# The last recurrent head of a hybrid decoder layer: from seven block sizes one at a time to two block sizes per step

## The chip, the core and the metric

The kernel runs on one core of a Trainium2 chip. The core has five engines that each take their instructions strictly in the order in which the program lists them: TensorE (PE, with its weight loads shown apart as PEld), VectorE (DVE), ScalarE (ACT), GpSimd (POOL) and SyncE (SP, which here issues the DMAs). They meet only through semaphores: an instruction that needs another engine's result waits at the head of its own queue, and everything behind it waits too. The metric is the device time of one execution in microseconds (us), here the median of three runs.

## The reference

One layer of batch 1, 1024 positions, width 1024, all in float32: a norm, one projection `h @ w_in` into attention (8 heads of 64) and a recurrence (4 heads of 128), an output projection, a norm and residual, and a feed-forward block of 4096. The part that matters here is the recurrence of one head:

```python
def step(state, xs):
    qc, kc, vc, gc = xs
    b = jnp.cumsum(gc, axis=2)
    o_inter = jnp.einsum('bhtk,bhkv->bhtv', qc * jnp.exp(b), state)
    diff = b[:, :, :, None, :] - b[:, :, None, :, :]
    decay = jnp.exp(jnp.where(causal, diff, -jnp.inf))
    a = jnp.einsum('bhtk,bhsk,bhtsk->bhts', qc, kc, decay)
    o = o_inter + jnp.einsum('bhts,bhsv->bhtv', a, vc)
```

The decay between two positions depends on the channel, so `a` is no plain matrix product. A kernel can still make it from products if it joins neighbouring blocks: for blocks of c positions, the queries of the upper block carry the decay from the block's start, the keys of the lower block the decay to the block's end, and one product gives all pairs between the two. Doubling c from 1 to 64 gives every pair inside 128 positions.

## The kernel before

All large products use float32r operands in a high and a low part, three matmuls for one (lines 90 to 92). The kernel has three stages: the input projections with the four recurrent heads among them, the attention with the output projection, and the feed-forward block.

The order of the work is written out by hand. `hgrn_core(h)` (line 501) emits the recurrence of head h, and at chosen places calls `fill(ns)` (line 195), which takes that much work, by fixed prices, from a queue of generators. For heads 0 to 2 the queue holds the projections of the next recurrent head (`hgrn_ig`, `hgrn_qf`); for the last head, h = 3, it holds the projections of attention pairs 0 and 1 (`attn_proj`, line 785). One item of those is three matmuls of 128x512, priced at 650; eight items make one half (512 positions) of a projection, in a PSUM bank of the tag "mm", of which there are two. `attn_proj(0)` yields the queries (tile `pm_aq`, two halves), the first half of the values (`pm_av`), the keys (`pm_ak`, two halves) and the second half of the values.

What an item leaves to the other engines matters below. A finished half is read out of PSUM by DVE (`qf` at line 806, `vf` at line 823, `kf` at line 740), and ACT and POOL split it into a high and a low part (lines 733 and 734), which SP sends on by DMA (lines 750, 811 and 812). The weights of the next projection are split by ACT (`wh`, line 86) and DVE (`wl`, line 87). The values are turned by four PE transposes (`pvt`, line 773), which need `vf`; ACT and DVE read the result (lines 776 and 777).

Inside `hgrn_core`, `qt` and `kt` are the queries and keys of the head (channels x positions), `tot` the decays of the blocks, `at` the matrix `a` of each 128 positions, and `pd` two ones-products for its diagonal (line 510). There are two ways to climb the block sizes:

- Heads 0 to 2 take three steps with c = 1, 4 and 16 (lines 520 to 571), each doing the sizes c and 2c. `quarter_sets` (line 472) prepares for each half of the positions a tile `qs` of 192 columns per 128 positions, by two ACT copies (lines 483 and 487) and two DVE products (lines 488 and 490). Eight matmuls of 128x192 (`pl`, line 529) go to four PSUM banks, DVE scales `qt` and `kt` and multiplies the decays (lines 542 to 556), prepares the next sets, and then writes `at` by twelve predicated copies (line 561). After each step come two fills of 3500. Size 64 follows as eight matmuls of 64x64 (line 572) and two DVE products.
- The last head takes the seven sizes of `LEVELS` one at a time (lines 585 to 613): eight matmuls of 128x64 (line 593), one DVE product each for `kt` (line 597) and `qt` (line 599), the decays (line 603), one predicated copy for all of `at` (line 604), and a fill of 3700, 2900 or 2200.

All fills of the last head are multiplied by the `scale` of 1.15 that is handed to it. After the sizes the keys are transposed (`pk`, line 615), the state is carried (`pu`, `st`) and the output formed (`po`).

A float32 product counts as two PE instructions, so eight of them are 16 in the trace.

Of the kernel before, what the change touches and what calls it, by code (L numbers as in the profile page):

```python
# [37 lines left out]
def hymba_layer(ctx, tc, x, w_in, w_out, w_ff1, w_ff2, g_pre, lb_logits, g_mix, g_post,  # L38
# [156 lines left out]
    def fill(ns, least=False):  # L195
        debt[0] += ns
        if least:
            debt[0] = max(debt[0], 1.0)
        while debt[0] > 0 and queue:
            try:  # L200
                cost = next(queue[0])
            except StopIteration:
                queue.pop(0)
                continue
            if cost is None:
                break
            debt[0] -= cost
        debt[0] = min(debt[0], 0.0)
# [292 lines left out]
    def hgrn_core(h, scale, after=None):  # L501
        hd = heads[h]
        inat, gate, prod, qt, kt, tot = (hd[n] for n in ("inat", "gate", "prod", "qt", "kt", "tot"))
        ready = quarter_sets(hd, h, 0, tot) if h < HH - 1 else None
        fill((5900 if 0 < h < HH - 1 else 5200) * scale)
        at = slab("S", f"at{h}", F32, (P, NT, P))
        for hf in range(2):
# [7 lines left out]
            nc.sync.dma_start(out=gcols, in_=g_mix.rearrange("(k p) -> p k", p=P))  # L515
        if h == HH - 1:
            load_bias(0)
        if h < HH - 1:
            fill(1200 * scale)
            totals = slab("P", f"tot{h}")  # L520
            for step in range(3):
                c = 4 ** step
                nb = 32 // c
                sets, cv = ready
                banks4 = []
                for u in range(4):
                    pl = bank(("s", "t", "pv")[(2 * step + u // 2) % 3], f"pl{h}_{step}{u}").rearrange("p (n q) -> p n q", n=2)
                    for n in range(2 * u, 2 * u + 2):
                        TE.matmul(pl[:, n % 2, :192], kt[:, n * P:(n + 1) * P], sets[u // 2][:, n % 4],  # L529
                                  start=True, stop=True)  # L530
                    banks4.append(pl)
                w = T // (4 * c)
                at_ = (0, 768, 960)[step]
                tots = totals[:, at_:at_ + 3 * w].rearrange("p (i w) -> p i w", i=3)
                u23, u123, nx = (tots[:, i] for i in range(3))
                cw = cv.rearrange("p n b f -> p (n b) f")
                q4 = qt.rearrange("p (m f c) -> p m f c", f=4, c=c)
                k4 = kt.rearrange("p (m f c) -> p m f c", f=4, c=c)

                def spread(ap, k=c):  # L540
                    return ap.unsqueeze(2).to_broadcast([P, w, k])
                V.tensor_tensor(out=q4[:, :, 1], in0=q4[:, :, 1], in1=spread(cw[:, :, 0]), op=ALU.mult)
                for hf in range(2):
                    n4 = slice(hf * 4, hf * 4 + 4)
                    V.tensor_tensor(out=qt[:, hf * 512:hf * 512 + 512].rearrange("p (n b f c) -> p n b (f c)", n=4, f=4, c=c)
                                    [:, :, :, 2 * c:],
                                    in0=sets[hf][:, :, 128:].rearrange("p n (b w) -> p n b w", b=nb),
                                    in1=cv[:, n4, :, 0:1].to_broadcast([P, 4, nb, 2 * c]), op=ALU.mult)
                V.tensor_tensor(out=u23, in0=cw[:, :, 2], in1=cw[:, :, 3], op=ALU.mult)
                V.tensor_tensor(out=u123, in0=cw[:, :, 1], in1=u23, op=ALU.mult)  # L550
                V.tensor_tensor(out=nx, in0=cw[:, :, 0], in1=u123, op=ALU.mult)
                if step < 2:
                    ready = quarter_sets(hd, h, step + 1, nx)
                V.tensor_tensor(out=k4[:, :, 2], in0=k4[:, :, 2], in1=spread(cw[:, :, 3]), op=ALU.mult)
                V.tensor_tensor(out=k4[:, :, 1], in0=k4[:, :, 1], in1=spread(u23), op=ALU.mult)
                V.tensor_tensor(out=k4[:, :, 0], in0=k4[:, :, 0], in1=spread(u123), op=ALU.mult)
                for u, pl in enumerate(banks4):
                    for part_, mask, c2 in ((0, masks[:, 2 * step], c), (2, masks[:, 2 * step + 1], 2 * c),
                                            (1, near[:, step], 2 * c)):
                        av = at[:, 2 * u:2 * u + 2].rearrange("p n (b two c) -> p n b two c", two=2, c=c2)  # L560
                        V.copy_predicated(
                            av[:, :, :, 1, :],
                            mask.rearrange("p (b c) -> p b c", c=c2).unsqueeze(1).to_broadcast([P, 2, 64 // c2, c2]),
                            pl[:, :, part_ * 64:part_ * 64 + 64].rearrange("p n (b c) -> p n b c", c=c2))
                cur = nx
                table_part()
                fill(3500 * scale)
                table_part()
                fill(3500 * scale)
            pl = bank("s", f"pl{h}_6")  # L570
            for n in range(NT):
                TE.matmul(pl[:64, n * 64:(n + 1) * 64], kt[:, n * P:n * P + 64], qt[:, n * P + 64:(n + 1) * P],
                          start=True, stop=True)
            S.activation(at[:64, :, 64:], pl[:64].rearrange("p (n c) -> p n c", n=NT), AF.Copy)
            kv, qv = (x.rearrange("p (n two c) -> p n two c", two=2, c=64) for x in (kt, qt))
            cv = cur.rearrange("p (n two) -> p n two", two=2)
            V.tensor_tensor(out=qv[:, :, 1], in0=qv[:, :, 1], in1=cv[:, :, 0:1].to_broadcast([P, NT, 64]), op=ALU.mult)
            V.tensor_tensor(out=kv[:, :, 0], in0=kv[:, :, 0], in1=cv[:, :, 1:2].to_broadcast([P, NT, 64]), op=ALU.mult)
            nx = tp.tile([P, NT], F32, tag="tot8", name=f"tot{h}_8", bufs=1)
            V.tensor_tensor(out=nx, in0=cv[:, :, 0], in1=cv[:, :, 1], op=ALU.mult)  # L580
            cur = nx
            fill(3400 * scale)
        else:
            cur = tot
            fill(1200 * scale)
            for li, c in enumerate(LEVELS):
                nb = 64 // c
                qv = qt.rearrange("p (b two c) -> p b two c", two=2, c=c)
                kv = kt.rearrange("p (b two c) -> p b two c", two=2, c=c)
                av = at.rearrange("p n (b two c) -> p n b two c", two=2, c=c)  # L590
                pl = bank("s", f"pl{h}_{li}")
                for n in range(NT):
                    TE.matmul(pl[:, n * 64:(n + 1) * 64], kt[:, n * P:(n + 1) * P],
                              qv[:, n * nb:(n + 1) * nb, 1, :], start=True, stop=True)
                w = T // (2 * c)
                cv = cur[:, :2 * w].rearrange("p (b two) -> p b two", two=2)
                V.tensor_tensor(out=kv[:, :, 0, :], in0=kv[:, :, 0, :],
                                in1=cv[:, :, 1:2].to_broadcast([P, w, c]), op=ALU.mult)
                V.tensor_tensor(out=qv[:, :, 1, :], in0=qv[:, :, 1, :],
                                in1=cv[:, :, 0:1].to_broadcast([P, w, c]), op=ALU.mult)  # L600
                nx = slab("P", f"tot{h}_{w}") if w > 32 else \
                    tp.tile([P, w], F32, tag=f"tot{w}", name=f"tot{h}_{w}", bufs=1)
                V.tensor_tensor(out=nx[:, :w], in0=cv[:, :, 0], in1=cv[:, :, 1], op=ALU.mult)
                V.copy_predicated(
                    av[:, :, :, 1, :],
                    masks[:, li].rearrange("p (b c) -> p b c", c=c).unsqueeze(1).to_broadcast([P, NT, nb, c]),
                    pl.rearrange("p (n b c) -> p n b c", n=NT, c=c))
                cur = nx
                fill((3700 if li == 0 else 2900 if li < 3 else 2200) * scale)
        ktr = slab("T", f"ktr{h}", F32, (P, NT, P))  # L610
        for hf in range(2):
            pt = bank("t", f"pk{h}_{hf}")
# [1699 lines left out]
```

## Time and profile before

| what | value |
|---|---|
| median of 3 runs | 1205.58 us (1205.57 to 1205.9) |
| the profiled execution, from outside | 1205.52 us |
| its span, first to last instruction | 1203.5 us |
| outside the span | 2.0 us |
| mean granted TensorE clock | 0.999 |
| the last head, from its `pd` to the end of its `pu` | 249.5 to 292.6 us |

Times inside the span count from its first instruction. A row of a timeline has the start, the length, the engine, the source line, the operation with the tile that it writes and the tiles that it reads, the shape and the count; an ending in brackets is the idle time before it and what ended that. Ends of matmuls are modelled and overlap the next one's start, so what a matmul costs is read from start to start.

### The profile page before, as it was taken

What the parts mean: (1) busy time and instruction counts of PE and PEld (TensorE: products, weight loads), DVE (VectorE), ACT (ScalarE), POOL (GpSimd) and SP (SyncE); (2) the same over time, 40 slices, a digit from 0 to 9 for tenths busy, and PEclk for the clock granted to TensorE, in tenths of its full rate; (3) what the DMA queues carried; (4) which work ended last, traced back from release to release, by engine and by line L of the source; (5) the groups of instructions that cost most, each with busy time, mean ns of one, the idle gap of its engine ahead of it and who ended that gap; (6) DMA issues with size and microseconds to landing.
All of it is one profiled execution on the core that took longest, in us unless ns stands there. A gap on an engine that the chain in (4) does not pass through costs nothing.

```text
span 1203.5 us, 17310 instructions
## 1 busy us (share of the span) xinstructions
PE 1195.3 (99%) x6342; PEld 1025.7 (85%) x6342; DVE 849.7 (71%) x1438; ACT 542.3 (45%) x1065; POOL 294.7 (24%) x280
## 2 busy tenths in 40 slices
PE   9999999999999999999999999999999999999997
PEld 9898989888888888888888888888888888888886
DVE  5696978775666767676599665766687553578796
ACT  7633333321565668855664222222234543434562
POOL 0121112010111110153421787575531000000022
PEclk9999999999999999999999999999999999999999
DMA  5222323135545556272524465553587534523337
GB/s 218 71 68 84 96 85 95 50 100 123 156 107 129 130 150 153 57 244 103 192 75 163 165 229 184 182 206 135 201 326 269 183 105 140 173 89 105 105 105 279
DMA packets 90547, 175.46 MB, mean 146 GB/s; under 512 B 14944, under 2 KB 42464, under 8 KB 90464
## 3 DMA queue, kind: packets, MB, share of 16 engines
q1 hardware_dynamic: 90320, 174.37, 45.6%
q8 instruction: 50, 0.82, 0.3%
q14 instruction: 33, 0.27, 0.1%
q10 hardware_dynamic: 144, 0.00, 0.0%
HBM read 116.91 MB, written 47.99 MB: 137 GB/s over the span
## 4 chain that ended last, share of the span: by engine, by line
PE 96%; ACT 2%; DVE 1%; issue 1%; DMA 0%; POOL 0%; DVEq 0%; POOLq 0%; ACTq 0%
PE f L2052 18%; PE f2s L2052 7%; PE pig L92 2%; PE pig L90 2%; PE pig L91 2%; PE pl L529 2%; PE pwo L90 2%; PE pwo L92 2%; PE pwo L91 2%; PE pm_ak L90 1%; PE pm_aq L90 1%; PE pm_f L90 1%; PE pm_aq L92 1%; PE pm_ak L92 1%; PE pm_ak L91 1%; PE pm_aq L91 1%
## 5 line engine op out<-in xcount | busy, mean ns | idle before, releaser
L87 DVE TENSOR_TENSOR al<-ar,ah 128x1024 fp32r<-128x1024 f32 x56 | 70.6, 1261 | 80.4 <-ACT ah L86 80.2
L2052 PE MATMUL f<-bh,ah 128*128 128x512 f32 x320 | 124.5, 389 | 0.0
L2052 PE MATMUL f<-bl,ah 128*128 128x512 f32 x320 | 124.5, 389 | 0.0
L2052 PE MATMUL f<-bh,al 128*128 128x512 f32 x320 | 124.5, 389 | 0.0
L86 ACT ACTIVATE ah<-ar 128x1024 fp32r<-128x1024 f32 x56 | 59.1, 1056 | 86.6 <-DMA ar<-actd 84.3
L2052 PEld LDWEIGHTS f<-bl,ah 128*128 128x128 f32 x320 | 60.1, 188 | 12.6
L2052 PEld LDWEIGHTS f<-bh,al 128*128 128x128 f32 x320 | 60.1, 188 | 12.5
L2052 PEld LDWEIGHTS f<-bh,ah 128*128 128x128 f32 x320 | 60.1, 188 | 12.3
L2126 POOL TENSOR_SCALAR lbl<-ssq 128x1 f32<-128x1 f32 x4 | 3.3, 820 | 245.7 <-ACT fd L2122 245.5
L1675 POOL TENSOR_TENSOR e<-x,e 128x512 f32<-128x512 f32 x14 | 21.6, 1541 | 131.0 <-DVE x L1626 123.8
L2052 PE MATMUL f2s<-bl,ah 128*128 128x512 f32 (+1 forms) x128 | 48.9, 382 | 0.0
L2052 PE MATMUL f2s<-bh,al 128*128 128x512 f32 (+1 forms) x128 | 48.9, 382 | 0.0
L2052 PE MATMUL f2s<-bh,ah 128*128 128x512 f32 (+1 forms) x128 | 48.9, 382 | 0.0
L718 POOL TENSOR_SCALAR tout<-traw 128x256 f32<-128x256 f32 x16 | 18.4, 1150 | 107.0 <-DMA traw<-in_bias_tab_dram 107.0
L87 DVE TENSOR_TENSOR bl<-br,bh 128x1024 fp32r<-128x1024 f32 x32 | 40.1, 1253 | 1.3 <-ACT bh L86 1.2
L2069 ACT ACTIVATE acc<-f 128x512 f32<-128x512 f32 x28 | 16.7, 598 | 49.5 <-PE f L2052 49.5
L86 ACT ACTIVATE bh<-br 128x1024 fp32r<-128x1024 f32 x32 | 33.6, 1050 | 4.3 <-PE f L2052 2.7
L87 DVE TENSOR_TENSOR wl<-raw,wh 128x1024 fp32r<-128x1024 f32 x21 | 25.9, 1233 | 10.2 <-ACT wh L86 10.2
L764 POOL TENSOR_TENSOR kl<-kf,kh 64x512 fp32r<-64x512 f32 x12 | 15.4, 1287 | 70.9 <-ACT kh L763 49.4
L90 PE MATMUL pwo<-woh,mt 128*128 128x512 f32 x80 | 32.2, 402 | 0.0
L92 PE MATMUL pwo<-woh,mt 128*128 128x512 f32 x80 | 31.3, 391 | 0.0
L91 PE MATMUL pwo<-wol,mt 128*128 128x512 f32 x80 | 31.2, 390 | 0.0
(1724 smaller groups left out, 3937.7 us busy)
## 6 DMA issues: line engine op xcount, KB each, us to landing
ar<-actd SPq DMA_DIRECT2D x56, 512.0 KB, 3.6
br<-in_w_ff_dram SPq DMA_DIRECT2D x16, 1024.0 KB, 5.8
raw<-in_w_in_dram SPq DMA_DIRECT2D x28, 512.0 KB, 4.1
w1r<-in_w_ff_dram SPq DMA_DIRECT2D x14, 1024.0 KB, 6.5
actd<-e SPq DMA_DIRECT2D x17, 768.0 KB, 4.3
actd<-e SPq DMA_DIRECT2D x11, 1024.0 KB, 4.1
xr<-in_x_dram SPq DMA_DIRECT2D x8, 512.0 KB, 8.0
raw<-in_w_out_dram SPq DMA_DIRECT2D x8, 512.0 KB, 3.7
```

The lines of the kernel that those rows point to most:

```text
L86: S.activation(hi, src, AF.Copy)
L87: eng.tensor_tensor(out=lo, in0=src, in1=f32(hi), op=ALU.subtract)
L90: TE.matmul(dst, lhs[0], rhs[0], start=start, stop=False)
L91: TE.matmul(dst, lhs[0], rhs[1], start=False, stop=False)
L92: TE.matmul(dst, lhs[1], rhs[0], start=False, stop=stop)
L529: TE.matmul(pl[:, n % 2, :192], kt[:, n * P:(n + 1) * P], sets[u // 2][:, n % 4], start=True, stop=True)
L718: G.tensor_scalar(by_class(dst[:, part_ * w:(part_ + 1) * w]), in_blocks(raw[:, FAR * DIL:]), 8.0, None, op0=ALU.mult)
L764: G.tensor_tensor(out=kl[a:b], in0=src, in1=f32(kh[a:b]), op=ALU.subtract)
L1675: eng[0].tensor_tensor(out=e1[:, 3], in0=a21, in1=e1[:, 2], op=ALU.add)
L2052: TE.matmul(pm, a[:, j, c], b[:, j, d], start=start and j == 0 and q == 0, stop=stop and j == 1 and q == 2, skip_group_check=True)
L2069: S.activation(acc_at(p, i), pm, AF.Copy)
L2126: G.tensor_scalar(base[:, t:t + 1], sums[j][:, t:t + 1], 1.0 / D, EPS, op0=ALU.mult, op1=ALU.add)
```

## The change

The branch of the last head is taken out, and all four heads take three steps of two sizes, then size 64. The last head's `scale` goes from 1.15 to 1.0, so that its fills sum to 39400 where they were 38295. Lines move up by one inside the function and by 28 behind it; the body of the three steps is the same, only its indentation changes.

```diff
-        ready = quarter_sets(hd, h, 0, tot) if h < HH - 1 else None
+        ready = quarter_sets(hd, h, 0, tot)
         fill((5900 if 0 < h < HH - 1 else 5200) * scale)
...
-        if h < HH - 1:
-            fill(1200 * scale)
-            totals = slab("P", f"tot{h}")
-            for step in range(3):
...
-        else:
-            cur = tot
-            fill(1200 * scale)
-            for li, c in enumerate(LEVELS):
...
-                pl = bank("s", f"pl{h}_{li}")
-                for n in range(NT):
-                    TE.matmul(pl[:, n * 64:(n + 1) * 64], kt[:, n * P:(n + 1) * P],
-                              qv[:, n * nb:(n + 1) * nb, 1, :], start=True, stop=True)
...
-                cur = nx
-                fill((3700 if li == 0 else 2900 if li < 3 else 2200) * scale)
+        fill(1200 * scale)
+        totals = slab("P", f"tot{h}")
+        for step in range(3):
...
+            table_part()
+            fill(3500 * scale)
+            table_part()
+            fill(3500 * scale)
+        pl = bank("s", f"pl{h}_6")
...
+        fill(3400 * scale)
...
-        last_gate = hgrn_core(h, 1.15 if last else 1.0, open_attention if last else None)
+        last_gate = hgrn_core(h, 1.0 if last else 1.0, open_attention if last else None)
```

`table_part` has done all its parts in heads 0 to 2 and returns at once in the last head.

Three places show what this does to the queues. The first is ACT at the start of the last head, before the change (`texp` only fetches the table of the exponential, `wh_2742` are the weights of the first values):

```order
L1312 ACT_TABLE_LOAD
L1312 ACTIVATE texp<-nhalf 128x1
L86 ACTIVATE wh_2742<-raw_2499 128x1024
L469 ACTIVATE rc_2751<-rrow 128x512
L470 ACTIVATE rrow<-rc_2751 128x512
```

The same place after the change:

```order
L1284 ACT_TABLE_LOAD
L1284 ACTIVATE texp<-nhalf 128x1
L483 ACTIVATE qs_00_2726<-qt_2501 128x4x64
L487 ACTIVATE qs_00_2726<-qt_2501 128x4x32
L483 ACTIVATE qs_01_2731<-qt_2501 128x4x64
L487 ACTIVATE qs_01_2731<-qt_2501 128x4x32
L86 ACTIVATE wh_2752<-raw_2499 128x1024
```

Four copies for the first sets stand behind the table load and ahead of the weights.

The second place is DVE between the weights of the keys (`wl_2862`) and the turned values (`v_2830`), before the change:

```order
L87 TENSOR_TENSOR wl_2862<-raw_2607,wh_2861 128x1024
L597 TENSOR_TENSOR kt_2588<-kt_2588,tot_256_2849 128x128x4
L599 TENSOR_TENSOR qt_2501<-qt_2501,tot_256_2849 128x128x4
L603 TENSOR_TENSOR tot_128_2884<-tot_256_2849 128x128
L604 COPY_PREDICATED at_2778<-masks,pl_2_2873 128x128x4
L823 TENSOR_TENSOR vf_2890<-pm_av_2831,rrow 128x512
L777 TENSOR_TENSOR v_2830<-pvt_2909,v_2830 128x8x64
```

The same stretch after the change begins with the twelve copies of step 0, of which the last is shown; `vf_2945` ends it:

```order
L560 COPY_PREDICATED at_2781<-near,pl_03_2809 128x64x2
L778 TENSOR_TENSOR qf_2861<-pm_aq_2792,rrow 128x512
L87 TENSOR_TENSOR wl_2888<-raw_2607,wh_2887 128x1024
L541 TENSOR_TENSOR qt_2501<-qt_2501,tot_2799 128x64x4
L544 TENSOR_TENSOR qt_2501<-qs_10_2818,tot_2799 128x32x8
...
L555 TENSOR_TENSOR kt_2588<-kt_2588,tot_2799 128x64x4
L560 COPY_PREDICATED at_2781<-masks,pl_10_2893 128x32x4
...
L560 COPY_PREDICATED at_2781<-near,pl_13_2902 128x16x8
L795 TENSOR_TENSOR vf_2945<-pm_av_2871,rrow 128x512
L749 TENSOR_TENSOR v_2870<-pvt_2964,v_2870 128x8x64
```

Between `wl` and `vf` there are now 25 instructions of step 1 where there were four of one size, and `qf` and `wl` themselves stand behind all of step 0.

The third place is PE around the transposes of the values. Before the change:

```order
L90 MATMUL pm_ak_2896<-hTh_89,wh_2861 128x512
L91 MATMUL pm_ak_2896<-hTl_90,wh_2861 128x512
L92 MATMUL pm_ak_2896<-hTh_89,wl_2862 128x512
L773 MATMUL pvt_2909<-ident,vf_2890 128x128 x4
L593 MATMUL pl_3_2920<-qt_2501,kt_2588 128x64 x8
```

After it:

```order
L90 MATMUL pm_ak_2951<-hTh_89,wh_2887 128x512
L91 MATMUL pm_ak_2951<-hTl_90,wh_2887 128x512
L92 MATMUL pm_ak_2951<-hTh_89,wl_2888 128x512
L745 MATMUL pvt_2964<-ident,vf_2945 128x128 x4
L90 MATMUL pm_ak_2951<-hTh_91,wh_2887 128x512
```

The transposes still follow the fourth item of the keys; `pl_10` to `pl_13` of step 1 stand seven items ahead of them, three of the values and four of the keys.

More of the change, by code (lines that the diff above doesn't have):

```diff
@@ new lines, in hgrn_core @@
+        pl = bank("s", f"pl{h}_6")
+        for n in range(NT):
+            TE.matmul(pl[:64, n * 64:(n + 1) * 64], kt[:, n * P:n * P + 64], qt[:, n * P + 64:(n + 1) * P],
+                      start=True, stop=True)
+        S.activation(at[:64, :, 64:], pl[:64].rearrange("p (n c) -> p n c", n=NT), AF.Copy)
+        kv, qv = (x.rearrange("p (n two c) -> p n two c", two=2, c=64) for x in (kt, qt))
+        cv = cur.rearrange("p (n two) -> p n two", two=2)
+        V.tensor_tensor(out=qv[:, :, 1], in0=qv[:, :, 1], in1=cv[:, :, 0:1].to_broadcast([P, NT, 64]), op=ALU.mult)
@@ L610, in hgrn_core @@
+        V.tensor_tensor(out=kv[:, :, 0], in0=kv[:, :, 0], in1=cv[:, :, 1:2].to_broadcast([P, NT, 64]), op=ALU.mult)
+        nx = tp.tile([P, NT], F32, tag="tot8", name=f"tot{h}_8", bufs=1)
+        V.tensor_tensor(out=nx, in0=cv[:, :, 0], in1=cv[:, :, 1], op=ALU.mult)
+        cur = nx
+        fill(3400 * scale)
         ktr = slab("T", f"ktr{h}", F32, (P, NT, P))
```

118 lines of the change are left out of this document (42 added, 76 removed).

## Prediction

> **What bounds the kernel now.** The page's busy table, the clock row of its slices and its chain come first.
>
> ```profile
> span 1203.5 us, 17310 instructions
> ...
> PE 1195.3 (99%) x6342; PEld 1025.7 (85%) x6342; DVE 849.7 (71%) x1438; ACT 542.3 (45%) x1065; POOL 294.7 (24%) x280
> ...
> PE 96%; ACT 2%; DVE 1%; issue 1%; DMA 0%; POOL 0%; DVEq 0%; POOLq 0%; ACTq 0%
> ```
>
> PE is busy for 1195.3 of 1203.5 us and makes 96% of the chain. So a microsecond less of PE work is a microsecond gained, and any time in which PE waits is lost for good. The change must therefore be read twice: as PE work, and as queues on DVE, ACT and SP that PE waits for.
>
> **PE work.** From PE's timeline, start to start: one block of size c, one block of a two-size step, the block of size 64.
>
> ```profile
> 251.80 1.89 PE L593 MATMUL pl<-qt,kt 128*128 128x64 f32 x16
> 253.50 0.48 PE L90 MATMUL pm_aq<-hTh,wh 128*128 128x512 f32 x1
> ...
> 68.44 2.76 PE L529 MATMUL pl<-qs,kt 128*128 128x192 f32 x16
> 70.91 0.42 PE L90 MATMUL pig<-wig1h,hTh 128*128 128x256 f32 x1
> ...
> 98.98 1.15 PE L572 MATMUL pl<-qt,kt 128*64 128x64 f32 x16
> 100.06 0.50 PE L90 MATMUL pm_q<-hTh,wh 128*128 128x512 f32 x1
> ```
>
> Seven blocks of 253.50 - 251.80 = 1.70 go: 11.9 us. Three of 2.47 and one of 1.08 come: 8.5 us. PE saves **3.4 us**. The projection items are the same ones, only placed elsewhere.
>
> **The start of the last head.** The timelines of PE, its weight loads, DVE and ACT:
>
> ```profile
> 242.67 0.39 PE L90 MATMUL pm_aq<-hTh,wh 128*128 128x512 f32 x1
> 249.47 0.40 PE L510 MATMUL pd<-prh,ones 128*128 128x512 f32 x1
> 250.17 0.40 PE L510 MATMUL pd<-prl,ones 128*128 128x512 f32 x1
> ...
> 250.06 0.18 PEld L510 LDWEIGHTS pd<-prl,ones 128*128 128x128 f32 x1 [0.17 <-DVE prl L461]
> ...
> 249.32 0.69 DVE L461 TENSOR_TENSOR prl<-pr,prh 128x512 fp32r<-128x512 f32 x1
> ...
> 250.71 1.04 ACT L86 ACTIVATE wh<-raw 128x1024 fp32r<-128x1024 f32 x1
> ```
>
> Ten items stand between 242.67 and 249.47, 0.68 us each, and the last `pd` product already waits for `prl`, which DVE ends at 250.01. Everything up to `prl` stays as it is. The scale of 1.0 makes the first fill 5200, eight items of 650: PE comes to that product at 248.81 and starts it at 250.17 as before. **Stall 1.4**.
>
> Two items later (251.8) the first block needs the sets. Four ACT copies now start where `wh` started, at 250.71. Head 2 shows their pitch, 1.30 for four:
>
> ```profile
> 187.80 0.42 ACT L483 ACTIVATE qs<-qt 128x256 f32<-128x256 f32 x1
> 189.10 1.05 ACT L86 ACTIVATE wh<-raw 128x1024 fp32r<-128x1024 f32 x1
> ...
> 189.88 0.43 DVE L490 TENSOR_TENSOR qs<-qs,tot 128x256 f32<-128x256 f32 x1
> ```
>
> The second copy ends at 251.46, DVE's product 0.43 later, so PE starts at 252.1. **Stall 0.3**. The block ends at 254.6, and eleven items bring PE to 262.1. `wh` ends at 253.05.
>
> **Step 0 on DVE.** The same step in head 2, by the starts of its parts:
>
> ```profile
> 192.55 0.62 DVE L542 TENSOR_TENSOR qt<-qt,tot 128x256 f32<-128x256 f32 x1
> 199.21 0.92 DVE L561 COPY_PREDICATED at<-masks,pl 128x128 f32<-128x128 uint8 x2
> 204.14 0.45 DVE L542 TENSOR_TENSOR qt<-qt,tot 128x256 f32<-128x256 f32 x1
> 209.01 0.61 DVE L561 COPY_PREDICATED at<-masks,pl 128x128 f32<-128x128 uint8 x2
> 212.44 0.42 DVE L542 TENSOR_TENSOR qt<-qt,tot 128x256 f32<-128x256 f32 x1
> 213.98 0.42 DVE L554 TENSOR_TENSOR kt<-kt,tot 128x256 f32<-128x256 f32 x1
> 218.45 1.22 DVE L267 TENSOR_TENSOR gate<-gate,sg 128x1024 f32<-128x1024 f32 x1
> ```
>
> Step 0 takes 6.7 us to the last `kt` and 4.9 for its copies; step 1 4.9 and 3.4; step 2 4.5 from its first `kt` to its last copy. In heads 0 to 2 the work between the steps is read out by ACT, so that DVE may run late. In the last head it is read out by DVE itself.
>
> ```profile
> 251.78 1.23 DVE L87 TENSOR_TENSOR wl<-raw,wh 128x1024 fp32r<-128x1024 f32 x1 [1.77 <-ACT wh L86]
> 254.72 1.53 DVE L597 TENSOR_TENSOR kt<-kt,tot 128x512 f32<-128x512 f32 x1
> ...
> 254.41 1.28 POOL L734 TENSOR_TENSOR qf<-qf,hiq 128x512 fp32r<-128x512 f32 x1 [11.02 <-ACT hiq L733]
> ```
>
> `wl`, `qf` and the two `at` products take 2.94, so step 0 starts on DVE at 253.1 + 2.9 = 256.0. The `kt` row shows another delay: under POOL's subtraction, which ends at 255.69, a product of two SBUF tiles ended only 0.56 after it. After the change that subtraction lies over the first `qt` product of step 0, some 0.5 more than head 2 had. `kt` is ready at 256.0 + 6.7 + 0.5 = 263.2, the copies end at 268.1. PE starts step 1 at 263.4 instead of 262.1: **1.3**. Its fourth product needs the bank of `pl_01`, free after half the copies, at 265.9 instead of 265.25: **0.7**. Three more items bring PE to 268.7.
>
> **Keys and values.** `qf`, then ACT's `hiq`, then its `wh`, then `wl` stand behind the copies:
>
> ```profile
> 259.41 0.63 ACT L733 ACTIVATE hiq<-qf 128x512 fp32r<-128x512 f32 x1 [5.08 <-DVE qf L806]
> 259.95 1.04 ACT L86 ACTIVATE wh<-raw 128x1024 fp32r<-128x1024 f32 x1
> ...
> 266.88 0.68 DVE L823 TENSOR_TENSOR vf<-pm_av,rrow 128x512 f32<-128x512 f32 x1
> 268.14 0.60 PE L773 MATMUL pvt<-ident,vf 128*128 128x128 f32 x4
> ```
>
> `qf` ends at 268.8, `wh` at 268.9 + 0.54 + 1.04 = 270.5, so the keys start at 270.6 instead of 268.7: **1.9**. `wl`, held by POOL too, ends at 272.1 where the third matmul comes at 271.1: **1.1**. PE reaches the transposes at 274.5. Before, `vf` ended 0.6 us ahead of them; now it stands behind the whole of step 1: 272.0 + 4.9 + 3.4 = 280.3 at the latest, 279.9 without POOL's share, plus 0.68. PE waits to 280.9: **6.4**.
>
> **Behind the transposes** the chain is paid once more, in DMAs. SP's timeline, and the line of the key transfers:
>
> ```profile
> 274.76 2.64 SPq L750 DMA_DIRECT2D kh<-hik  x4
> 277.50 2.59 SPq L750 DMA_DIRECT2D kl<-kf  x4
> ...
> DMA to landing us min/median/max: 2.5/2.6/3.3
> ```
>
> Count from the start of step 2 on PE. DVE's `kt` products begin at 2.8, the copies end at 7.3, `kf` at 7.95, `hik` at 8.65. Four transfers of `hik` take SP to 11.3, the last landing at 13.3; four of `kf` follow, landed at 16.0. The program makes the second `kf` wait for the first four, since they read its buffer, and the second `hik` for the other four. So the second `kf` ends at 13.9, two products behind it bring `kt` for `pk` at 15.2 where PE comes at 14.45 (**0.8**); the second `hik` ends at 16.65, behind it `at` and `wh` at 18.2 where PE needs it at 16.8 (**1.5**), `wl` at 19.4 (**0.7**); and the next `vf` waits for transfers that land at 21.2 (**0.3**). Before the change the keys came earlier against their transfers and nothing of this showed. Unlike the sums above this has no like in head 2; its bounds are 0 (transfers earlier) and 5 (landing 3.3, as the slowest row).
>
> **The clock.** The last matmul, and the stretches behind it:
>
> ```profile
> 1197.24 0.28 PE L2052 MATMUL f2tail<-bh,al 128*128 128x256 f32 x1
> ...
> 1200.00:1201.00 1.00, 0.00 (x0) 0.00 (x0) 0.51 (x1) 0.00 (x0) 0.00 (x0) 0.78 0.29 109
> 1201.00:1202.00 1.00, 0.00 (x0) 0.00 (x0) 0.00 (x0) 0.00 (x0) 0.00 (x0) 0.50 1.04 385
> ```
>
> A share of 0.78 means a drop to 0.50 at 1200.56, 3.0 us after PE ended. The gap before `pvt` is twice that, so PE should come out of it at half speed. No row shows a return. If it takes 3.0 us of work as the drop took 3.0 of rest, **1.5** are lost; the bounds are 0 and 3. The Trainium skill, "TensorE: Matmul & The Clock Gate", Part 1, says that the clock is halved after an idle window of about 3.4 us and restored after a busy one of the same length. By that estimate 1.7 us would be lost instead of 1.5, and the forecast would be 0.2 later; this trace agrees on the drop, none shows the return.
>
> **Sum.** -3.4 + 1.4 + 0.3 + 1.3 + 0.7 + 1.9 + 1.1 + 6.4 + 0.8 + 1.5 + 0.7 + 0.3 + 1.5 = +14.5. The profiled execution took 1205.52 us, 2.0 outside its span and within 0.1 of the median, so the forecast is **1220.0 us**. Two items that move forward from the attention to this head cost nothing: the order is the same again from the 48th attention step on, and PE stays covered there by the same items.
>
> **Rivals.**
> - *Faster: DVE keeps up.* Only PE's 3.4 us count: 1202.1. It speaks for it that the same three steps run in heads 0 to 2 without a PE wait. The point that decides is `vf` before `pvt`: DVE would have to end step 1 6 us sooner than its lengths in head 2 add up to. That needs its rows to be that much too long, or PE work ahead of `pvt` that I missed. Chance 0.06.
> - *The two nearly cancel:* the stall at `pvt` alone is half its size, the rest hidden: within 2.4 us of before. Chance 0.05.
> - *Only the first half:* everything up to `pvt`, with clean DVE lengths, but no clock loss and no waits for transfers: -3.4 + 13.1 - 1.4 = +8.3, so 1213.8, some 1211 to 1216. Chance 0.28.
> - *All of it:* 1216 to 1224. Chance 0.53.
> - *More:* the attention's opening is late too, since DVE and SP enter it behind: over 1224. Chance 0.08.
> - *The change does not do what it says:* it speaks of about the same work between the steps. On PE that holds, eleven items or 7.5 us; on DVE a step brings 11.6 and 8.3 us, more than the 10 us of block and items that PE gives it in step 0. That is the forecast's own reason, not a further case.
>
> **Range and chances.** 1211 to 1224 leaves out the two small-effect cases and the late one, 0.19. A measurement of this kernel can tell some 0.2% (2.4 us) from no change. Faster 0.06, same 0.05, slower 0.89.
>
> **What would show it.** In the changed profile: PE idle of about 1.4 at `pd` behind `prl`; 2 to 3 before the keys behind `wh`; over 5 at `pvt` behind `vf`, with DVE in copies without a gap ahead of it; a stretch at clock 0.5 after that; and waits of 0.5 to 1.5 at `pk` and the next queries. It would be wrong if `pvt` shows no wait; too long if DVE's step 1 takes under 7 us; too short if waits go on past the last head.

## The result, and the profile after

The changed kernel takes **1222.07 us** (median of four runs, 1221.87 to 1222.72), the kernel before in the same session 1205.74 (1205.57 to 1206.46). The ratio is 1.0135, with a 95% interval of 1.0118 to 1.0153: 16.3 us slower. Forecast were 1220.0, with a range of 1211 to 1224.

The page of the changed kernel, the lines that answer to those of before:

```profile
span 1220.8 us, 17273 instructions
...
PE 1200.4 (98%) x6294; PEld 1024.9 (84%) x6294; DVE 856.0 (70%) x1488; ACT 546.1 (45%) x1078; POOL 295.3 (24%) x280
...
PE 90%; DVE 4%; ACT 3%; issue 1%; DMA 1%; SPq 0%; POOL 0%; DVEq 0%; POOLq 0%; ACTq 0%
```

The program has 48 matmul records less (seven blocks of 16 have become four), and PE is busy 5.1 us longer. So some of the same matmuls have become slower. PE is now idle for 1220.8 - 1200.4 = 20.4 us, where it was 8.2. PE's share of the chain falls from 96% to 90%; DVE's rises from 1% to 4% and ACT's from 2% to 3%.

The view of PE's waits between 240 and 330 us has no row for the kernel before. For the changed one it has ten (engine, line, what it waited for, us in total, times, longest):

```profile
PE pvt L745 <- DVE vf L795: 4.6, 1, 4.6
PE pm_ak L90 <- ACT wh L86: 1.6, 1, 1.6
PE pm_aq L90 <- ACT wh L86: 1.0, 1, 1.0
PE pl L528 <- DVE kt L555: 0.9, 1, 0.9
PE pm_ak L92 <- DVE wl L87: 0.8, 1, 0.8
PE pd L510 <- ACT prh L459: 0.6, 1, 0.6
PE pm_aq L92 <- DVE wl L87: 0.5, 1, 0.5
PE pk L587 <- DVE kt L577: 0.4, 1, 0.4
PE pl L528 <- DVE at L560: 0.3, 1, 0.3
PE pd L510 <- DVE prl L461: 0.2, 1, 0.2
```

All ten lie at places that the prediction named. Two that it named have no row: the first block, and the second `vf`. At `pd` it expected the wait behind `prl`; the longer part, 0.6, is behind ACT's `prh`. What a wait costs is a little more than its idle time, because a matmul's record lasts 0.39 while the next one could start after 0.23. So the costs below go from start to start. The rows of PE's timeline that they come from:

```profile
262.13 0.39 PE L92 MATMUL pm_av<-hTh,wl 128*128 128x512 f32 x1
263.45 2.19 PE L528 MATMUL pl<-qs,kt 128*128 128x192 f32 x12 [0.93 <-DVE kt L555]
...
268.55 0.39 PE L92 MATMUL pm_av<-hTh,wl 128*128 128x512 f32 x1
270.51 0.50 PE L90 MATMUL pm_ak<-hTh,wh 128*128 128x512 f32 x1 [1.57 <-ACT wh L86]
270.84 0.40 PE L91 MATMUL pm_ak<-hTl,wh 128*128 128x512 f32 x1
271.99 0.79 PE L92 MATMUL pm_ak<-hTh,wl 128*128 128x512 f32 x1 [0.75 <-DVE wl L87]
...
275.50 0.39 PE L92 MATMUL pm_ak<-hTh,wl 128*128 128x512 f32 x1
280.47 1.12 PE L745 MATMUL pvt<-ident,vf 128*128 128x128 f32 x4 [4.58 <-DVE vf L795]
...
284.80 0.56 PE L92 MATMUL pm_ak<-hTh,wl 128*128 128x512 f32 x1
285.19 2.76 PE L528 MATMUL pl<-qs,kt 128*128 128x192 f32 x16
```

Step 1's block starts 263.45 - 262.13 - 0.23 = 1.1 us late, the keys 268.55 to 270.51, less 0.23, 1.7 late, and `pvt` 4.7. DVE's timeline shows what was done meanwhile:

```profile
270.49 1.45 DVE L87 TENSOR_TENSOR wl<-raw,wh 128x1024 fp32r<-128x1024 f32 x1 [1.64 <-ACT wh L86]
...
278.80 0.61 DVE L560 COPY_PREDICATED at<-masks,pl 128x128 f32<-128x128 uint8 x2
279.45 0.29 DVE L560 COPY_PREDICATED at<-near,pl 128x128 f32<-128x128 uint8 x1
279.72 0.69 DVE L795 TENSOR_TENSOR vf<-pm_av,rrow 128x512 f32<-128x512 f32 x1
282.25 0.69 DVE L749 TENSOR_TENSOR v<-pvt,v 128x512 fp32r<-128x512 f32 x1 [1.84 <-ACT v L748]
```

`vf` has no idle time directly in front of it: the product that it reads ended at 268.9 on PE, and then it stood for 10.8 us in DVE's queue (268.9 to 279.72). First came the keys' `wl`, for which DVE itself was idle for 1.64 us, since ACT's `wh` stood behind the `hiq` of a `qf` that step 0's copies had held up until 268.13. Then came the whole of step 1, products and copies, without a gap. `vf` ends at 280.41, and PE starts 0.06 later.

The clock has its own row. The windows view, in windows of 3.41 us whose ends lie on the grid on which the granted clock changes (in order: length, busy time of PE, its weight loads, DVE, ACT and POOL, clock, DMA share, GB/s):

```profile
247.59:251.00 3.41, 2.60 (x10) 1.60 (x10) 2.84 (x6) 2.13 (x4) 0.00 (x0) 1.00 0.30 83
...
268.07:271.48 3.41, 1.60 (x6) 0.67 (x4) 1.77 (x3) 1.57 (x2) 1.27 (x1) 1.00 0.18 38
271.48:274.90 3.42, 2.91 (x7) 2.33 (x8) 3.11 (x10) 1.12 (x4) 0.00 (x0) 0.50 0.72 162
274.90:278.31 3.41, 0.99 (x5) 0.47 (x3) 3.23 (x12) 0.00 (x0) 0.00 (x0) 1.00 0.27 109
278.31:281.72 3.41, 1.25 (x5) 1.25 (x6) 2.00 (x6) 0.10 (x1) 0.00 (x0) 0.50 0.03 7
281.72:285.14 3.42, 3.42 (x9) 2.65 (x8) 2.15 (x7) 0.50 (x1) 0.00 (x0) 0.50 0.36 72
...
302.20:305.62 3.42, 1.92 (x8) 1.17 (x8) 1.23 (x1) 2.03 (x4) 1.00 (x1) 1.00 0.71 138
305.62:309.03 3.41, 3.41 (x12) 2.72 (x11) 0.69 (x1) 0.00 (x0) 0.00 (x0) 0.50 1.05 196
```

There are three stretches at half clock, not one: before `pvt`, around and behind it, and a last one from 305.6 that follows no wait longer than 1 us. A matmul of 128x512 takes 0.43 there instead of 0.23.

### The profile page after: what moved, and what is told of

Same layout as the page of the kernel before. It is cut to its first block, busy times and chain, and to the rows that moved or that the text cites. A ratio compares the mean times of both kernels' runs of the same rounds, so it can differ in the third digit from the quotient of the medians.

```text
span 1220.8 us, 17273 instructions
## 1 busy us (share of the span) xinstructions
PE 1200.4 (98%) x6294; PEld 1024.9 (84%) x6294; DVE 856.0 (70%) x1488; ACT 546.1 (45%) x1078; POOL 295.3 (24%) x280
## 4 chain that ended last, share of the span: by engine, by line
PE 90%; DVE 4%; ACT 3%; issue 1%; DMA 1%; SPq 0%; POOL 0%; DVEq 0%; POOLq 0%; ACTq 0%
PE f L2024 18%; PE f2s L2024 7%; PE pig L92 2%; PE pig L90 2%; PE pig L91 2%; PE pl L528 2%; PE pwo L92 2%; PE pwo L90 2%; PE pwo L91 2%; PE pm_ak L90 1%; PE pm_aq L92 1%; PE pm_f L90 1%; PE pm_ak L91 1%; PE pm_ak L92 1%; PE pm_aq L90 1%
## 5 line engine op out<-in xcount | busy, mean ns | idle before, releaser
L2041 ACT ACTIVATE acc<-f 128x512 f32<-128x512 f32 x28 | 16.8, 598 | 50.4 <-PE f L2024 50.4
L528 PE MATMUL pl<-qs,kt 128*128 128x192 f32 x192 | 33.6, 327 | 1.3 <-DVE kt L555 0.9
L560 DVE COPY_PREDICATED at<-masks,pl 128x128 f32<-128x128 uint8 x96 | 33.5, 349 | 1.6
L528 PEld LDWEIGHTS pl<-qs,kt 128*128 128x128 f32 x192 | 31.2, 191 | 2.6 <-issue 1.9
```

The lines of the kernel that those rows point to most:

```text
L560: V.copy_predicated(av[:, :, :, 1, :], mask.rearrange("p (b c) -> p b c", c=c2).unsqueeze(1).to_broadcast([P, 2, 64 // c2, c2]), pl[:, :, ...
L2041: S.activation(acc_at(p, i), pm, AF.Copy)
```

## The experiments

Eleven kernels, in four groups. Each time is a median of 4 to 11 runs; the ratio stands against the kernel before of the same session (1205.35 to 1205.65).

| run | what | median us | ratio (95%) |
|---|---|---|---|
| a_copies_late | copies behind the step's first fill | 1212.29 | 1.0053 (1.0041 to 1.0066) |
| a_turn6 | `pvt` three items later | 1217.40 | 1.0103 (1.0088 to 1.0118) |
| a_pd | two items moved ahead of `pd` | 1217.64 | 1.0103 (1.0087 to 1.0118) |
| a_scale115 | new loop, scale 1.15 | 1228.92 | 1.0193 (1.0179 to 1.0207) |
| b_scale100 | old loop, scale 1.0 | 1220.64 | 1.0126 (1.0112 to 1.0140) |
| b_pd | old loop, first fill 5200 | 1208.32 | 1.0023 (1.0014 to 1.0031) |
| a_warm_pvt | idle matmuls in `pvt`'s bank | 1226.96 | 1.0174 (1.0160 to 1.0188) |
| a_warm_t | idle matmuls in a free bank | 1220.76 | 1.0125 (1.0108 to 1.0142) |
| a_warm_all | the same in three waits | 1220.31 | 1.0120 (1.0107 to 1.0134) |
| a_fills | items dealt out anew | 1211.68 | 1.0051 (1.0039 to 1.0064) |
| a_order | that, and DVE's order | 1206.23 | 1.0004 (0.9995 to 1.0013) |

### DVE's queue: is it the order, or the amount of work?

**a_copies_late.** The same instructions, the read-outs ahead of the copies:

```diff
-            copies()
             cur = nx
             table_part()
             fill(3500 * scale)
+            copies()          # last head only; the other heads as before
             table_part()
             fill(3500 * scale)
```

> The changed kernel, with the twelve predicated copies of each step of the last head issued behind the first of the two fills of the step instead of ahead of it. The same instructions, in another order on DVE: qf and vf stand ahead of the copies. Theory (read-outs wait in DVE's queue): qf ends at about 264 instead of 268.8, so the keys' wh is there when PE comes and that wait (1.7) goes, about 0.7 stays at wl; vf ends at about 275.3 instead of 280.4, so pvt starts 5.2 us sooner with a wait of about 3. Gain 5.2, and up to 2 more if the clock then stays up: expected 1216, within 1214.5 to 1217.5. Rival (DVE's total work bounds this stretch, the order does not matter): within 1 us of the changed kernel, 1221 to 1223.

Measured 1212.29: 9.8 us gained, from the order alone. That is more than expected, and below the range. Two of the three stretches at half clock went with the waits; the one behind `pvt` is left (275.03 to 278.45). Of PE's waits between 240 and 330 us five rows are left where ten were; the three behind `pd`:

```profile
PE pvt L750 <- DVE vf L800: 2.4, 1, 2.4
PE pl L528 <- DVE kt L555: 0.9, 1, 0.9
PE pl L528 <- DVE at L561: 0.7, 2, 0.4
```

Those at `pd` and at the blocks stay; of the waits of the fills and turns behind step 1's block only the one at `pvt` is left. `pvt` starts at 275.00 instead of 280.47, and the waits at the keys, at `pk` and at the next queries are gone; the last two the expectation had left standing. The rival (amount, not order) falls.

**a_turn6 and a_pd** leave DVE's order alone and move PE's work around it.

```diff
-                if n == 3 and hf == 0:
+                if hf == 0 and n == (6 if pr == 0 else 3):
                     values_turn()
```

> The changed kernel with the first value transposes behind the seventh key item instead of the fourth, directly ahead of step 2's block. Theory (vf is late because it stands behind step 1 on DVE, whatever PE does): pvt starts at 280.4 as before, after a wait shorter by three items, about 2.7 us, and step 2's block starts up to 3.9 us sooner, since the three items no longer run behind pvt at half clock; 1219.0, within 1217.5 to 1220.5. Rival (the rest of the head is set by DVE's later work): no gain, 1221.5 to 1222.5.

```diff
-        fill((5900 if 0 < h < HH - 1 else 5200) * scale)
+        fill((6500 if h == HH - 1 else 5900 if h > 0 else 5200) * scale)
...
-        fill(3400 * scale)
+        fill((2100 if h == HH - 1 else 3400) * scale)
```

> The changed kernel with two fill items more ahead of the pd products of the last head and two less ahead of pk (first fill 6500 instead of 5200, the fill behind the size-64 block 2100 instead of 3400). The 1.3 us at pd go. If the prediction's terms add up as PE waits, everything behind moves up by 1.3, pvt too, to 279.1, and the time is 1220.8. If DVE's queue is what counts from its first wl to vf, the keys still start at 270.5 and pvt at 280.4, and the gain comes out behind pvt: 1.4 us for two items that are already done, and up to 2.3 more because the keys then end two items sooner, ahead of the transfers that the next queries wait for: 1218.5, within 1217 to 1220.

PE's timelines, first a_turn6, then a_pd:

```profile
270.29 0.50 PE L90 MATMUL pm_ak<-hTh,wh 128*128 128x512 f32 x1 [1.56 <-ACT wh L86]
...
280.25 0.66 PE L745 MATMUL pvt<-ident,vf 128*128 128x128 f32 x4 [3.87 <-DVE vf L795]
```

```profile
270.41 0.50 PE L90 MATMUL pm_ak<-hTh,wh 128*128 128x512 f32 x1 [2.92 <-ACT wh L86]
...
280.36 1.12 PE L745 MATMUL pvt<-ident,vf 128*128 128x128 f32 x4 [4.52 <-DVE vf L795]
```

With three items more ahead of it, and with the 1.3 us at `pd` gone, the keys start at 270.3 and 270.4 and `pvt` at 280.25 and 280.36: where they started in the changed kernel (270.51 and 280.47), to 0.2. From DVE's first `wl` at 253.3 to `vf` DVE's queue sets the pace, together with ACT's `hiq` and `wh`, for which it waits 1.64 us. What PE saves ahead of `pvt` turns into a longer wait there (2.92 at the keys instead of 1.57) and comes out only as work that is already done behind it. The gains are 4.7 us (a_turn6) and 4.4 (a_pd), and they arise behind `pvt`. In a_turn6 the item behind step 2's block starts at 284.89 instead of 287.66, since the three items are already done, and the stretch at half clock from 305.6 doesn't come: 2.8 and 1.6. In a_pd the keys end two items sooner, and the waits at `pk` and at the next queries are gone, and with them the last stretch at half clock.

### The scale and the number of items

```diff
-        last_gate = hgrn_core(h, 1.0 if last else 1.0, open_attention if last else None)
+        last_gate = hgrn_core(h, 1.15 if last else 1.0, open_attention if last else None)
```

> The change's loop with the scale left at 1.15. Theory (the wait at the first value transposes comes from vf being issued behind step 1's DVE work): with 1.15 the value projection's eight items all stand ahead of step 1, so vf stands ahead of step 1's products and pvt waits for nothing. The wait at pd (1.3 us) goes too. The keys still start behind the second wh at about 270.5, because that hangs on step 0's DVE work alone, so the PE wait there grows from 1.7 to about 4 us with three items more done before it. Step 2's block then starts about 281 with five items more done: 8 us gained. Expected 1214, within 1211 to 1217. Rival (the loop's DVE work as such is too much, wherever vf stands): no more than the 1.3 us at pd comes back, 1220 to 1221.

The wait at `pvt` went, as the theory says, and so did the one at `pd`; the wait at the keys grew to 3.6. But the run was 7 us slower than the changed kernel, with a wide range (1224.8 to 1230.3). Two of PE's waits between 240 and 330 us, and below them the row of DVE's timeline that stands behind the first, name what was missed:

```profile
PE ps_N L873 <- DVE stat L878: 3.0, 1, 3.0
PE pm_ak L90 <- DVE v L749: 2.6, 1, 2.6
```

```profile
319.08 0.69 DVE L778 TENSOR_TENSOR qf<-pm_aq,rrow 128x512 f32<-128x512 f32 x1 [8.27 <-DMA q<-hiq]
```

`v` now stands behind step 1's copies, and the second half of the keys needs the bank that `v` frees. And all fills of the head grow by 15% (together from 39.4 to 45.3 thousand of the planner's units, some 9 items more), so the next pair's second `qf` comes up while DVE still has to wait for that pair's earlier query transfers, 8.3 us. The attention's first sums and its first `stat` are queued behind it on DVE, and `ps_N` on PE waits for them. The expectation had looked no further than step 2. The trace is of the fastest of the five runs (1224.79); what the others lost beyond it isn't shown.

```diff
-        last_gate = hgrn_core(h, 1.15 if last else 1.0, open_attention if last else None)
+        last_gate = hgrn_core(h, 1.0 if last else 1.0, open_attention if last else None)
```

> The old loop over seven block sizes with the scale at 1.0. Theory: the only certain cost is the wait at the last pd product, 1.3 us; the sizes' DVE work of some 3 us each is shorter than the 4 to 5.6 us of PE work that stand between two blocks, and vf stands behind one short size only, so nothing else waits for long. Expected 1207.3, within 1206 to 1209. Rival (the scale alone makes the loss, by taking PE cover from DVE everywhere): 1215 or more.

Also wrong, by 13 us: 1220.64, nearly the time of the changed kernel, for another reason. Hardly anything is lost in the head, but the old loop's fills lose 13% of their items, and the third pair's keys come too late for the attention: the last transfer of their high part `kh` goes out at 413.18 us, before at 397.3. PE's waits from 330 us on, the first two rows:

```profile
PE ps_N L901 <- DMA kh<-kh: 3.9, 3, 3.0
PE ps_N L902 <- DMA kl<-kl: 1.3, 2, 0.9
```

With the third row, 1.0 at `ps_D`, PE is idle for 6.2 us behind key transfers, and a stretch at half clock follows the longest of these waits (415.91 to 419.33). That is about half of the 15 us; the rest lies in smaller waits and wasn't taken apart.

So the scale isn't a knob for the wait at `pd`: it also says how much of the projections is left for the attention. Over the whole head the fills come to 33.3 thousand times 1.15, or 38.3 thousand, before; to 39.4 thousand in the changed kernel, where the new fills make up for the scale; and to 33.3 thousand here, some 8 items less. **b_pd** takes the one fill alone:

```diff
-        fill((5900 if 0 < h < HH - 1 else 5200) * scale)
+        fill(5900 if 0 < h < HH - 1 else 5200)
```

> The kernel before with the first fill of the last head at 5200 instead of 5980 and everything else at the scale of 1.15: two items fewer ahead of pd. Theory (the loss of the old loop at scale 1.0 came from the items that the later fills lost, which put the second pair's keys too late for the attention): here only the wait at pd of 1.3 us comes in, 1206.9, within 1206.2 to 1208.2. Rival (the first fill is what made that loss): 1215 or more.

1208.32, just over the upper end. The wait at `pd` is there (0.6 and 0.2 idle), and one of 1.0 at `pt_F` in the attention, whose order the two items shift. The 15 us of b_scale100 don't come from the first fill.

### The clock

> The changed kernel with 18 more matmuls of 128x512 in the bank of the first value transposes, in the time in which PE waits for vf anyway (18 x 0.227 = 4.1 us in a wait of 4.7). They compute nothing that is used. Theory (the clock is set by how busy PE was in the window before): the stretch at half clock behind pvt, nine matmuls and the transposes, goes: 2.1 us gained, 1220.0, within 1219.4 to 1220.6; the stretch at 305 to 309 stays, since its window holds other waits. Rival (what follows is set by DVE and the key transfers, not by PE's clock): the 2.1 us come back as longer waits at pk and the next queries, within 0.5 us of the changed kernel.

The edit, between `pvt`'s bank and its transposes:

```diff
         pt = bank(tag, f"pvt{pr}{hf}")
+        if pr == 0 and hf == 0:
+            for n in range(18):
+                TE.matmul(pt, part(hT, 0, 0)[0][:, :P], part(hT, 0, 0)[0], start=True, stop=True)
```

It became 4.9 us slower than the changed kernel. The experiment missed its aim, and its row says why:

```profile
281.65 6.48 PE L746 MATMUL pvt<-hTh 128*128 128x512 f32 x18 [5.89 <-DVE vf L798]
```

The bank of `pvt` is the one that `vf` reads. So the matmuls waited for `vf` themselves, and then ran on the path. **a_warm_t** puts them into a bank of another tag that is free:

```diff
+            warm = bank("t", "warm")
+            for n in range(18):
+                TE.matmul(warm, part(hT, 0, 0)[0][:, :P], part(hT, 0, 0)[0], start=True, stop=True)
```

> The changed kernel with 18 matmuls of 128x512, whose product nothing uses, between the fourth key item and the first value transposes, this time in a bank of their own that is free there, so that they can run while PE waits for vf (18 x 0.227 = 4.1 of 4.7 us). Theory (the half clock behind pvt comes from PE's rest ahead of it and costs PE time that nothing hides): no stretch at 0.50 between pvt and step 2's block, which starts about 2.1 us sooner after pvt; 1220.0, within 1219.0 to 1220.8. Rival (what follows is set by DVE and the key transfers): the 2.1 us come back as longer waits at pk and the next queries, 1221.5 to 1222.5.

1220.76, inside the range, but not by the way expected: the stretch at 0.50 behind `pvt` is still there. In this execution neither the first nor the last stretch came. From the first key matmul PE took 1.3 us less to the place, and the 18 matmuls ended 1.8 us ahead of `vf`. **a_warm_all** therefore fills three waits (at the keys, ahead of `pvt` and at the next pair's queries), with 6, 25 and 4 matmuls:

```diff
+    def warm(name, n, tag="t"):
+        wb = bank(tag, f"warm{name}")
+        for i in range(n):
+            TE.matmul(wb, part(hT, 0, 0)[0][:, :P], part(hT, 0, 0)[0], start=True, stop=True)
...
+        if pr == 0 and hf == 0:
+            warm("p", 25)
...
+        if pr == 1:
+            warm("q", 4, "pv")
...
+        if pr == 0:
+            warm("k", 6)
```

> The changed kernel with matmuls of 128x512 whose product nothing uses in three of its PE waits, each in a bank that is free: 6 ahead of the first keys (1.4 us in a wait of 1.7), 25 ahead of the first value transposes (5.7), 4 ahead of the next pair's queries (0.9 in 1.1). Theory (the half clock is decided by how busy PE was in the window before, and costs 2.1 us behind pvt and 1.7 in the last stretch): no stretch at 0.50 between 260 and 310; 1218.3, within 1217.3 to 1219.7. Rival (the half clock costs nothing, since DVE and the transfers set the pace): 1221.5 to 1222.5.

The windows view of a_warm_all, one window:

```profile
260.00:310.00 50.00, 46.10 (x229) 36.64 (x228) 31.61 (x84) 8.51 (x15) 3.88 (x3) 1.00 0.43 99
```

The clock stays at 1.00 throughout, and the time is 1220.31: 1.8 us gained by the medians, 2.4 by the two spans (1218.4 and 1220.8), where 3.8 were expected; the time lies above the range and below the rival's. PE's timeline shows most of the 3.7 at the place itself and a wait that takes part of it back:

```profile
305.87 0.66 PE L752 MATMUL pvt<-ident,vf 128*128 128x128 f32 x4 [0.47 <-DVE vf L804]
306.36 1.73 PE L595 MATMUL pu<-inat,ktr 128*128 128x128 f32 x14
```

`pu` starts at 306.36 where it was 309.00, 2.6 sooner. Its `pvt` would have followed the item of 305.01 directly, but waits for the second `vf`. So the half clock is worth some 2 us of this result, not 3.8.

### All of it at once

**a_fills** deals the items out anew, **a_order** adds DVE's order:

```diff
-        fill((5900 if 0 < h < HH - 1 else 5200) * scale)
+        fill((6500 if last_ else 5900 if h > 0 else 5200) * scale)
...
-            fill(3500 * scale)
+            fill(fa * scale)       # last head: 2850, 2200, 4150
+            copies(0, (4, 2, 4)[step])       # a_order only
...
-            fill(3500 * scale)
+            fill(fb * scale)       # last head: 4800, 3500, 2200
+            copies((4, 2, 4)[step], 4)       # a_order only
...
-        fill(3000 * scale)
+        fill((1700 if last_ else 3000) * scale)
...
+            if pr == 0 and hf == 1:       # a_order only
+                w_get(A0 + 1)
             full = half(f"qf{pr}{hf}", F32R)
```

> The changed kernel with its work in another order in the last head, nothing left out: two items more ahead of pd, 12 and 9 and 10 items behind the three steps (fills 2850 and 4800, 2200 and 3500, 4150 and 2200), two items less ahead of the sums (1700 instead of 3000); the keys' weights are split ahead of the second qf; the copies of a step stand behind its first fill, in step 1 half of them behind its second. Theory: every wait of the changed profile comes from a read-out that stands behind a step's work on DVE or from too few items between two steps, so all of them can go at once: no PE wait over 0.7 between pd and the last po, no half clock there, and the 3.4 us of PE work come out as far as the attention leaves them: 1204.5, within 1203.2 to 1206.5, so about level with the kernel before or a little under it. Rival (DVE's total work in this stretch is the bound): not under 1209.

> The same numbers of items as in the run before this one (fills 6500; 2850 and 4800, 2200 and 3500, 4150 and 2200; 1700), but copies and weights where the changed kernel has them. Theory: the wait at pd goes and vf, now issued ahead of step 1, no longer makes pvt wait; the keys still start at about 270.4, since the second qf stands behind step 0's copies, so PE waits there for 3 to 4 us and loses clock behind it; the second half of the keys waits some 2 us for the bank that v frees behind step 1's copies. 1210.5, within 1208.5 to 1213. Rival (the number of items between the steps is all that counts): the same as the run with the new order, 1204 to 1206.

a_fills came to 1211.68 and a_order to 1206.23, both within what was expected. a_order gives back 15.8 of the 16.3 us with nothing left out, and is level with the kernel before: 1.0004, the interval on both sides of 1. It has no half clock in the head, but two waits over the 0.7 that were allowed for:

```profile
PE pl L529 <- DVE at L562: 1.8, 2, 1.5
PE pl L529 <- DVE kt L556: 1.1, 2, 0.9
```

They are what keeps the 3.4 us of PE work from showing: with the copies later, step 1's block waits for the banks that they free (1.8), and steps 1 and 2 for `kt` (1.1). In this stretch DVE's amount of work does become the bound, but 5.5 us below a_fills: from `wl` at 253.26 to the last product of step 2 before its copies (282.80) DVE has no gap over 0.2 us. No version that was found beats the kernel before.

## Why the prediction came out right, and where its steps were off

**The way was right**: DVE reads out the last head's fill items, so that steps which bring DVE's work in long pieces put `qf`, `wl` and `vf` behind them, and PE waits. a_copies_late shows it, since nothing but DVE's order differs there. That the new work between the steps is the same on PE and not on DVE stood in the prediction's last rival.

**Term by term**, in us:

| term | predicted | measured |
|---|---|---|
| PE work | -3.4 | -3.3 |
| `pd` | 1.4 | 1.3 |
| first block | 0.3 | 0.2 |
| step 1's `kt` | 1.3 | 1.1 |
| bank of `pl_01` | 0.7 | 0.7 |
| keys' `wh` | 1.9 | 1.7 |
| keys' `wl` | 1.1 | 0.9 |
| half clock ahead of `pvt` | none | 1.5 |
| `pvt` | 6.4 | 4.7 |
| half clock behind `pvt` | 1.5 | 2.1 |
| `pk`; queries' `wh`, `wl`; second `vf` | 0.8; 1.5; 0.7; 0.3 | 0.5; 1.1; 0.7; 0 |
| half clock from 305.6 | none | 1.6 |
| sum | 14.5 | 14.8 |

The measured column is the difference of starts in the two traces: the four blocks take 8.6 us (2.57, 2.47, 2.47 and 1.08, the second without its bank wait) where the seven took 11.9; `pd`'s four products take 2.28 us (248.31 to 250.59) instead of 0.94, the block with the bank of `pl_01` 3.13 (263.45 to 266.58) instead of 2.47; the seven matmuls ahead of `pvt` 3.05 (271.99 to 275.04) instead of 1.6; from `pvt` to the next block 4.72 (280.47 to 285.19) instead of 2.60; and the last stretch 3.39 (305.61 to 309.00) instead of 1.8.

- *DVE's lengths* from head 2 held: step 0 took 7.1 us to the last `kt` (256.20 to 263.30; 6.7 and 0.5 for POOL predicted), step 1 4.5 and 3.5 for its copies (4.9 and 3.4).
- *The sums agree in part by luck.* The half clock behind `pvt` came to 3.7 us where 1.5 stood in the sum, 2.2 more. The waits, with the 1.5 of half clock ahead of `pvt` counted into the one there, came out 2.0 us shorter than written, none of them by more than 0.4.
- *`pvt`* starts at 280.47 where 280.9 was given. PE came there at 275.73, not 274.5, because the clock had already dropped at 271.5. So the wait is shorter than the 5 us that were to show it, and the 1.5 of half clock ahead of it cost nothing: they lie in the time until `vf`. The rows of both belong together (6.2 against 6.4).
- *The sum up to `pvt` is one term, not seven.* It came out right because `pvt` was reckoned along DVE. But the prediction wrote the stalls at `pd`, at step 1 and at the keys as costs that add up. a_pd took the first away, and the keys and `pvt` started where they had.
- **The clock was mis-sized**, and its mechanism was wrong. The prediction had one drop, 3.0 us after PE comes to rest, and a return after 3.0 us of work: 1.5 us. The 3.0 us, read off at the kernel's end (1197.52 to 1200.56), are no constant: the same drop came 2.4 us after PE's last matmul in the changed kernel (1214.53 to 1216.97) and 4.9 in b_scale100 (1213.12 to 1218.05). The runs show windows of fixed length and three drops: 2.1 and 1.6 us in the open, beside 1.5 that lie in the time until `vf`. a_warm_all, without any of them, came out 1.8 us lower, so that about half of the 3.7 is the clock's own price; part of the rest came back as a wait for the second `vf`.
- *What is missing from the sum.* The first product of the FFN's second half (line 2052 before, 2024 after) starts at 909.4 where it was 892.4, of which 0.2 lie ahead of the last head (its first `pm_aq` at 242.87 and 242.67): 16.8, and 14.8 are accounted for. Some 0.3 us are restarts: the matmul behind a wait takes 0.33 to the next instead of 0.23, at 270.51, 303.32 and 304.58. And two waits in the attention are new, which was to be "covered by the same items"; from start to start they cost 1.1 us:

```profile
468.14 0.44 PE L953 MATMUL pt_F<-ident,pf 128*128 128x128 f32 x2 [0.43 <-ACT pf L931]
...
470.65 0.44 PE L953 MATMUL pt_F<-ident,pf 128*128 128x128 f32 x2 [0.32 <-ACT pf L931]
```

The "all of it" rival thus held. The restarts and the attention were not in it, and the terms ahead of `pvt` were each up to 0.2 too long; the errors partly cancel, and the forecast was 2 us low. Open stays some 0.6 us.

## What to carry to other kernels

Where an engine's in-order queue both does the serial work of a loop and reads out the work that is meant to fill its gaps, longer steps delay the filler, however equal the amounts are on the other engine: issue the read-outs ahead of whatever can wait (9.8 us here, from moving the twelve copies of each step behind a fill). Stalls on one engine that come from another's queue don't add up: reckon along the queue that sets the end. Removing a stall ahead of the last one moved nothing there (a_pd: the keys and `pvt` kept their starts); its 4.4 us came out behind `pvt`, where less was left to do. And a number that deals out filler work is felt wherever that work would otherwise have stood: 13% less cost the old loop 15 us, most of it in the attention far behind the edit, and 15% more cost the new one 7.

## What the runs showed of the hardware that was not expected

**The clock is decided in windows of 3.41 us that run on their own.** Every change in the changed kernel lies on one grid: 271.48, 274.90, 278.31, 285.14, 305.62, 309.03, with distances of 3.41 or 3.42, twice that (6.83) and six times that (20.48). The Trainium skill, "TensorE: Matmul & The Clock Gate", Part 1, has this: windows of 3413 ns that run free. The runs agree to 0.01.

**A window need not be idle.** The table of windows above shows what went ahead of each drop: PE busy for 1.60, 0.99 and 1.92 of 3.41 us, that is 47, 29 and 56%. At 2.60 (76%) the clock stayed. Other runs put the border near a half, and not sharp: 1.57 us were followed by a drop in a_warm_t, in a_scale115 1.61 were not and 1.86 were. In no run here did a drop follow a window with 2.08 us (61%) or more. The same part of the Trainium skill speaks of an idle window. Here one wait of 1.0 us and one of 0.5 within one window, with their restarts, were enough for the stretch from 305.6.

```profile
277.70:281.11 3.41, 1.57 (x10) 1.00 0.01 2
281.11:284.52 3.41, 3.41 (x10) 0.50 0.38 75
```

These are PE's windows in a_warm_t (length, busy, clock, DMA share, GB/s): half busy, then at half clock. Since the grid doesn't start with the kernel, the same waits may or may not cost a stretch: in a_turn6 and a_warm_t the one at 271.5 didn't come, with the same waits ahead of it. Where the stretches lie is known only for the traced execution of each kernel; over the four runs of the changed kernel the mean clock was 0.993 to 0.995.
